# One decoder layer in split fp32r on one core: the seven-product form for the two halves of token chunk 0 in the gate and up projections

## The chip, the cores and the metric

The kernel runs on one core of a Trainium2 chip. The metric is device time in microseconds of one launch, the median of the runs, lower is better. Engines are named as in the profile: PE is TensorE's matmul, PEld its weight load, DVE is VectorE, ACT is ScalarE, POOL is GpSimd, and SP is SyncE, which issues nearly all DMAs here. A DVE instruction, for instance, is one row in DVE's own queue, and each engine runs its queue in order.

## The reference, cut to what matters

A decoder layer for 1024 prompt tokens and 8 x 4 sample tokens, width 1024. The change is in its two SwiGLU blocks; between them stand a gated-delta group, sliding-window attention and a projection, which stay as they are.

```python
def swiglu(h, w_gate, w_up, w_down):
    return (jax.nn.silu(h @ w_gate) * (h @ w_up)) @ w_down

h = rmsnorm(x, lw['norm_ffn1_pre'])
x = x + 0.5 * rmsnorm(swiglu(h, lw['ffn1_w_gate'], lw['ffn1_w_up'], lw['ffn1_w_down']), lw['norm_ffn1_post'])
...                                        # the mixing part
h = rmsnorm(x, lw['norm_ffn2_pre'])
x = x + 0.5 * rmsnorm(swiglu(h, lw['ffn2_w_gate'], lw['ffn2_w_up'], lw['ffn2_w_down']), lw['norm_ffn2_post'])
gate = jax.nn.sigmoid(x @ lw['ple_gate'])  # then the per-layer embedding
```

w_gate and w_up are 1024 x 2816, w_down is 2816 x 1024, all float32.

## The kernel before

**Tiling.** The 1056 tokens lie as columns in three chunks: chunk 0 has 288, chunks 1 and 2 have 384 each. The model width is eight row tiles of 128 (k = 0 to 7). Weights are the stationary operand, 128 x 128 at a time, and tokens the moving one. To keep float32 accuracy every operand is split into a high and a low fp32r half (`hhi`/`hlo` for tokens, the two halves of a `wsp` tile for weights), and a product takes three matmuls: high x high, high x low, low x high (`mm3` at L136 to L138, `mm3p` at L353 to L355). The splitting of weights is one cast on ACT (L128) and one subtraction on DVE (L129) for each 128 x 1024.

**Gate and up (`ffn_up`).** The 2816 output rows are eleven groups of 256, that is two tiles j = 0, 1 of 128. Group 0 is done for all three chunks the plain way (`classic`: 24 matmuls for a chunk, a tile j and a weight). Then chunks 1 and 2 are turned into the operands of a seven-product form (Winograd's variant of Strassen's) of a 2 x 2 block product: the blocks are the two halves of k, the two tiles j, and the two chunks as the two column halves. `half_sums` makes the token sums: in place in chunk 2's upper half of k, and in three tiles `th`. For each later group and each weight, `units` loads 1 MB (`raw`) and makes four `wsp` tiles: the two plain ones and the sums; `seven` does seven products of 12 matmuls of 384 columns, 84 instead of 96, in three accumulators `a`, `b`, `c_` of the `ax` ring, with DVE and ACT adding up between. Chunk 0 goes beside them the plain way: 48 matmuls of 288 columns for each group and weight (`c0a`, `c0b`; banks of the `mm` ring, three of them). In the last group chunk 0 is left out of `seven` and done by `classic` at the end. Results go to `scr_h` in HBM (`out`, L399).

**Order.** The program is written in the order of the work; a scheduler lays the instructions of each engine out by priority and by what it expects to be ready, and each engine then runs its row strictly in order. The first feed-forward takes the chunks in the order 0, 1, 2, the second in 1, 2, 0. Loads and writes stand in one row on SP.

**Down (`ffn_down`).** For each chunk 22 tiles `gt` are read back from `scr_h` (the first ones in one piece, `ga`, the others through a ring `gr` of four) and split on ACT (L548) and DVE (L549); w_down is loaded and split on the way.

**Memory.** Pools lie on a stack. `fq`, `fp` and `th` belong to gate and up; `yd` and `gp` (with all 22 `gt`) take their place afterwards, so the first write to a tile there waits for the last user of what lay there before. A small pool `tp`, open all the time, holds norm temporaries.

Of the kernel before, what the change touches and what calls it, by code (L numbers as in the profile page):

```python
# [8 lines left out]
F32 = mybir.dt.float32  # L9
# [8 lines left out]
P = 128  # L18
GPB = 22
# [15 lines left out]
def emit(tc, A):  # L35
# [11 lines left out]
    tp = pool(name="tp", bufs=2)  # L47
# [167 lines left out]
    def apply_norm(c, x1, r, gain, H, hp=None):  # L215
# [3 lines left out]
        for d in range(KT):  # L219
            if hp and d % 2:  # L220
                hf = hp.tile([P, 384], F32, name=nm("hf"), tag="hfx", bufs=2)[:, :n]
# [4 lines left out]
            tt(lo[:, d, :], hf, hi[:, d, :].bitcast(F32), ALU.subtract)  # L226
# [132 lines left out]
    def half_sums(H, T, fp):  # L359

        (h1, l1), (h2, l2) = H[1], H[2]
        sgt = lambda: fp.tile([P, 384], F32, name=nm("hs"), tag="sg", bufs=SGB)
        for k in range(4):
            b12, b11, b22, b21 = [sgt() for _ in range(4)]
            for t, hh, ll, q in ((b12, h2, l2, k), (b11, h1, l1, k), (b22, h2, l2, k + 4), (b21, h1, l1, k + 4)):
                tt(t, f32(hh[:, q, :]), f32(ll[:, q, :]), ALU.add)
            t3, t2 = sgt(), sgt()
            tt(t3, b22, b12, ALU.subtract)
            tt(b12, b12, b11, ALU.subtract)
            tt(t2, b22, b12, ALU.subtract)  # L370
            tt(b21, b21, t2, ALU.subtract)
            S.copy(h2[:, k, :], b12)  # L372
            tt(l2[:, k, :], b12, f32(h2[:, k, :]), ALU.subtract)
            for i, t in enumerate((t2, t3, b21)):
                S.copy(T[i][:, 0, k, :], t)
                V.tensor_tensor(T[i][:, 1, k, :], t, f32(T[i][:, 0, k, :]), ALU.subtract)
            yield
# [3 lines left out]
    def ffn_up(H, wg, wu, fq, fp, scr, order, opent, hooks={}):  # L381
# [47 lines left out]
        T = opent()  # L429
        for _ in half_sums(H, T, fp):  # L430
            pass
        h0, h1, h2 = H[0], H[1], H[2]
        B = lambda h, o: (lambda k: (h[0][:, o + k, :], h[1][:, o + k, :]))
        TT = lambda i: (lambda k: (T[i][:, 0, k, :], T[i][:, 1, k, :]))
        b11, b21, t1, b22, c0a, c0b = B(h1, 0), B(h1, 4), B(h2, 0), B(h2, 4), B(h0, 0), B(h0, 4)
        n0 = CH[0][1]
# [17 lines left out]
        def seven(us, f, with0):  # L454
# [6 lines left out]
            a, b, c_ = [axbank()[:, :384] for _ in range(3)]  # L461
# [10 lines left out]
            u2 = f.tmp()  # L472
            tt(u2, s1, b, ALU.add)
            pr(c_, q12, 0, t1, True, True)
            pr(b, q34, 0, TT(1), False, True, True)
            u3 = f.tmp()
            tt(u3, s1, b, ALU.add)  # L477
            tt(u3, u3, c_, ALU.add)
            f.sum(1, 2, u3)
            pr(a, u0, 4, b21, False, True, True)  # L480
            f.direct(0, 1, a)
            pr(b, u1, 4, TT(2), False, True, True)
            tt(s1, s1, b, ALU.add)
            f.sum(1, 1, s1)
            pr(c_, q34, 4, b22, False, True, True)
            tt(u2, u2, c_, ALU.add)
            f.sum(0, 2, u2)

        for g in range(1, NG):
# [3 lines left out]
            class Gate:  # L493
                def tmp(self):
                    return sgt(1)

                def c0(self, j, ps):
                    sg[0, j] = sgt(0)
                    S.activation(sg[0, j], ps, AF.Silu)

                def direct(self, j, c, ps):
                    sg[c, j] = sgt(c)
                    S.activation(sg[c, j], ps, AF.Silu)

                def sum(self, j, c, t):
                    sg[c, j] = t
                    S.activation(t, t, AF.Silu)

            class Up:
                def tmp(self):  # L510
                    return fq.tile([P, 384], F32, name=nm("ut"), tag="ut", bufs=4)

                def c0(self, j, ps):
                    self.direct(j, 0, ps)

                def direct(self, j, c, ps):
                    tt(sg[c, j], sg[c, j], ps, ALU.mult)
                    out(sg[c, j], c, 2 * g + j)

                sum = direct  # L520

            for w, f in ((wg, Gate()), (wu, Up())):
                seven(units(raw(w, g)), f, g < NG - 1)
# [4 lines left out]
    def ffn_down(wd, gp, scr, order, yt, finish, after, wide, rate):  # L528
# [3 lines left out]
        def load_g(c):  # L532
# [8 lines left out]
            for f in range(NF):  # L541
                gt = gp.tile([P, 2, 384], F32R, name=nm("gt"), tag="gt")[:, :, :n]
# [105 lines left out]
    ycur[0] = ycur[1] = ypc.__enter__()  # L648
# [1184 lines left out]
```

## Time and profile before

| | us |
|---|---|
| median of 3 runs | 2372.03 (2371.21 to 2372.98) |
| the profiled execution | 2367.41 |
| its span | 2365.7 |
| PE busy | 2252.4 |
| gate and up of the first feed-forward, to its last matmul | to about 506 |
| gate and up of the second, to its last matmul | about 1450 to 1941 |

In the table times within the execution count from the start of the span. Matmuls are pipelined, so that the duration of one (0.33 us at 384 columns) is longer than the step from one start to the next; the step is what counts in a series. A row in which several instructions of one kind were merged (x6) runs from the start of the first to the end of the last. What stands in brackets at the end of a row is the idle time of the engine before it and what ended it. The profile's PEclk is the share of full clock that was granted to TensorE.

### The profile page before, as it was taken

Reading aid. Unit: us, or ns where it says so; the run is one execution under the profiler, and the core shown is the slowest. Engines: PE = TensorE matmul, PEld = TensorE weight load, DVE = VectorE, ACT = ScalarE, POOL = GpSimd, SP = SyncE. Lnnn points to the kernel's source line nnn. Section 1 sums busy time; section 2 is a strip of 40 time slices with the busy share of each in tenths; the row PEclk is TensorE's granted clock in tenths of the full one; section 3 lists DMA queues with packets and bytes.
Section 4 is the critical chain, followed back from the end, with each engine's and each line's share of the span. In section 5 each row is a group of like instructions: output and inputs, shape, how many; then the busy total and the mean of one; then the engine's idle time right before and its main releaser. Section 6 shows DMA issues by size and latency. Waiting matters only on the chain.

```text
span 2365.7 us, 36438 instructions
## 1 busy us (share of the span) xinstructions
PE 2252.4 (95%) x14212; PEld 2142.4 (91%) x14212; DVE 1421.6 (60%) x2992; ACT 920.9 (39%) x1862; POOL 78.4 (3%) x150
## 2 busy tenths in 40 slices
PE   7999999989999699979999998999999999999998
PEld 6999999989999698878888798999999999999876
DVE  6755555555775549992456578965555464746536
ACT  6323222245453335532335555332322233534421
POOL 0000000000000004220010000000000000000000
PEclk9999999999999799978999998999999999999999
DMA  6122222276554426645654366122222256545401
GB/s 238 65 100 79 72 79 78 86 224 211 196 176 157 125 70 199 199 132 162 181 168 126 100 215 219 58 77 86 73 69 76 77 191 202 186 153 168 148 19 56
DMA packets 312658, 313.16 MB, mean 132 GB/s; under 512 B 25929, under 2 KB 295313, under 8 KB 312470
## 3 DMA queue, kind: packets, MB, share of 16 engines
q1 hardware_dynamic: 312486, 310.84, 40.5%
q8 instruction: 112, 1.84, 0.3%
q14 instruction: 60, 0.49, 0.1%
HBM read 235.57 MB, written 77.81 MB: 132 GB/s over the span
## 4 chain that ended last, share of the span: by engine, by line
PE 77%; DVE 13%; DMA 5%; ACT 3%; issue 2%; SPq 0%; DVEq 0%; ACTq 0%; POOL 0%; POOLq 0%
PE ax L353 8%; PE ax L354 8%; PE ax L355 8%; PE mm L353 8%; PE mm L355 8%; PE mm L354 8%; PE mm L136 5%; PE mm L137 5%; PE mm L138 5%; DMA gr<-scr_h 3%; PE mm L1735 1%; PE mm L1731 1%; PE mm L1732 1%; DVE cy L1026 1%; PE ax L986 1%
## 5 line engine op out<-in xcount | busy, mean ns | idle before, releaser
L129 DVE TENSOR_TENSOR wsp<-raw,wsp 128x1024 fp32r<-128x1024 f32 (+1 forms) x290 | 342.1, 1181 | 282.1 <-ACT wsp L128 281.0
L128 ACT CAST wsp<-raw 128x1024 fp32r<-128x1024 f32 (+1 forms) x290 | 292.9, 1014 | 325.5 <-PE mm L355 184.8
L353 PE MATMUL mm<-gt,wsp 128*128 128x384 f32 (+1 forms) x1056 | 341.8, 324 | 14.6 <-ACT gt L548 7.3
L355 PE MATMUL mm<-gt,wsp 128*128 128x384 f32 (+1 forms) x1056 | 340.8, 323 | 1.7 <-DVE wsp L129 1.6
L354 PE MATMUL mm<-gt,wsp 128*128 128x384 f32 (+1 forms) x1056 | 341.5, 323 | 0.0
L136 PE MATMUL mm<-hhi,wsp 128*128 128x384 f32 (+1 forms) x784 | 264.8, 338 | 10.2 <-ACT po L779 8.7
L138 PE MATMUL mm<-hhi,wsp 128*128 128x384 f32 (+1 forms) x784 | 261.7, 334 | 13.3 <-DVE wsp L129 9.9
L137 PE MATMUL mm<-hlo,wsp 128*128 128x384 f32 (+1 forms) x784 | 264.3, 337 | 0.0
L353 PE MATMUL ax<-hhi,wsp 128*128 128x384 f32 x640 | 214.6, 336 | 3.8 <-ACT hhi L372 3.8
L354 PE MATMUL ax<-hlo,wsp 128*128 128x384 f32 x640 | 214.5, 335 | 0.1
L353 PEld LDWEIGHTS mm<-gt,wsp 128*128 128x128 f32 x1056 | 199.9, 189 | 15.6 <-ACT gt L548 12.7
L355 PE MATMUL ax<-hhi,wsp 128*128 128x384 f32 x640 | 213.9, 335 | 0.0
L355 PEld LDWEIGHTS mm<-gt,wsp 128*128 128x128 f32 x1056 | 199.8, 189 | 2.7 <-DVE wsp L129 2.3
L354 PEld LDWEIGHTS mm<-gt,wsp 128*128 128x128 f32 x1056 | 200.0, 189 | 0.8 <-DVE gt L549 0.3
L128 ACT CAST wsp<-st 128x1024 fp32r<-128x1024 f32 x80 | 84.2, 1053 | 268.5 <-PE ax L355 264.8
L354 PE MATMUL mm<-hlo,wsp 128*128 128x288 f32 x576 | 169.8, 295 | 0.0
L353 PE MATMUL mm<-hhi,wsp 128*128 128x288 f32 x576 | 169.8, 295 | 0.0
L355 PE MATMUL mm<-hhi,wsp 128*128 128x288 f32 x576 | 169.7, 295 | 0.0
L138 PEld LDWEIGHTS mm<-hhi,wsp 128*128 128x128 f32 x784 | 153.4, 196 | 15.9 <-DVE wsp L129 10.1
L136 PEld LDWEIGHTS mm<-hhi,wsp 128*128 128x128 f32 x784 | 153.7, 196 | 13.5 <-ACT po L779 9.5
L353 PE MATMUL ax<-th,wsp 128*128 128x384 f32 x480 | 161.1, 336 | 0.6 <-DVE sg L477 0.6
L354 PE MATMUL ax<-th,wsp 128*128 128x384 f32 x480 | 160.4, 334 | 0.0
(457 smaller groups left out, 4460.2 us busy)
## 6 DMA issues: line engine op xcount, KB each, us to landing
raw<-in_ffn_w_down_dram SPq DMA_DIRECT2D x48, 1024.0 KB
raw<-in_ffn_w_gate_dram SPq DMA_DIRECT2D x24, 1024.0 KB
raw<-in_ffn_w_up_dram SPq DMA_DIRECT2D x24, 1024.0 KB
raw<-in_ffn_w_down_dram SPq DMA_DIRECT2D x24, 768.0 KB
scr_h<-sg SPq DMA_DIRECT2D x88, 192.0 KB
gr<-scr_h SPq DMA_DIRECT2D x80, 192.0 KB
raw<-in_w_out_dram SPq DMA_DIRECT2D x12, 1024.0 KB
xr<-scr_x SPq DMA_DIRECT2D x12, 768.0 KB
```

The lines of the kernel that those rows point to most:

```text
L128: S.copy(hi, src)
L129: V.tensor_tensor(lo, src, hi.bitcast(F32), ALU.subtract)
L136: TE.matmul(ps, lhsT=wh, rhs=xh, start=(i == 0), stop=False)
L137: TE.matmul(ps, lhsT=wh, rhs=xl, start=False, stop=False)
L138: TE.matmul(ps, lhsT=wl, rhs=xh, start=False, stop=(i == n - 1))
L353: TE.matmul(ps, lhsT=wh, rhs=xh, start=(first and i == 0), stop=False, skip_group_check=on)
L354: TE.matmul(ps, lhsT=wh, rhs=xl, start=False, stop=False, skip_group_check=on)
L355: TE.matmul(ps, lhsT=wl, rhs=xh, start=False, stop=(last and i == n - 1), skip_group_check=on)
L986: TE.matmul(po[:, (kv * 2 + i) * 64:(kv * 2 + i + 1) * 64], lhsT=pSs[kv][:, i, b, :], rhs=vb[b][:, kv * 64:kv * 64 + 64], start=(b == kb0) ...
L1026: stt(y[:, :L], xb[:, j:j + L], scT[:, t, 24 + j:25 + j], y[:, :L], ALU.mult, ALU.add)
L1731: TE.matmul(pg[:m], lhsT=xh, rhs=u[:, 0, ks], start=(k == 0), stop=False)
L1732: TE.matmul(pg[:m], lhsT=xh, rhs=u[:, 1, ks], start=False, stop=False)
```

## The change

Chunk 0 gets the seven-product form too, with its two halves of 144 columns as the two column halves. `half_sums` makes its sums as well (in place in the second half's upper k, and in three small tiles), after those of chunks 1 and 2. `seven` runs over a list of operand sets, first the one of 384 columns, then the one of 144, product by product; the narrow set has its accumulators in the `mm` ring. This holds for groups 1 to 9; group 10 runs the wide set alone, and `whole_rows` gives chunk 0 its plain rows back for the `classic` at the end. Since the sums need memory, `tp` is closed during gate and up (after group 0) and opened again behind it, `bias_rows` moves behind the first down phase, the `gt` tiles lie in two pools of eleven (`gq` lowest, `gp` on top of `yd`), and the pools of the last part are laid out anew.

```diff
-GPB = 22
+GPB = 11
...
-    tp = pool(name="tp", bufs=2)
+    class Cur:
+        def open(self, name): ...
+        def close(self): ...
+    tp = Cur()
...
-    def half_sums(H, T, fp):
+    def half_sums(H, T, T0, fp):
+        for Ts, c1, o1, c2, o2, n in ((T, 1, 0, 2, 0, 384), (T0, 0, 0, 0, 144, 144)):
+            (h1, l1), (h2, l2) = H[c1], H[c2]
+            s1, s2 = slice(o1, o1 + n), slice(o2, o2 + n)
+            for k in range(4):
+                b12, b11, b22, b21 = [sgt() for _ in range(4)]
+                for t, hh, ll, q, sl in ((b12, h2, l2, k, s2), (b11, h1, l1, k, s1), (b22, h2, l2, k + 4, s2),
+                                         (b21, h1, l1, k + 4, s1)):
+                    tt(t, f32(hh[:, q, sl]), f32(ll[:, q, sl]), ALU.add)
...
+    def whole_rows(H, fp):
+        h, l = H[0]
+        a, b = slice(0, 144), slice(144, 288)
         for k in range(4):
...
+            tt(t, t, u, ALU.add)
+            S.copy(h[:, k, b], t)
+            tt(l[:, k, b], t, f32(h[:, k, b]), ALU.subtract)
...
+        SETS = [(384, axbank, operands(1, 0, 2, 0, 384, T)), (144, mmbank, operands(0, 0, 0, 144, 144, T0))]
...
-            pr(a, u0, 0, b11, True, True)
-            s1 = f.tmp()
-            S.copy(s1, a)
-            if with0:
-                for j, u in enumerate((u0, u1)):
-                    p0 = mmbank()[:, :n0]
-                    pr(p0, u, 0, c0a, True, False)
-                    pr(p0, u, 4, c0b, False, True)
-                    f.c0(j, p0)
-            pr(b, q12, 4, TT(0), True, True)
...
+            for (o, (a, b, c_), b11, b21, t1, b22, t2, t3, t4) in st:
+                pr(a, u0, 0, b11, True, True)
+                S.copy(o.s1, a)
+            for (o, (a, b, c_), b11, b21, t1, b22, t2, t3, t4) in st:
+                pr(b, q12, 4, t2, True, True)
+                tt(o.u2, o.s1, b, ALU.add)
+            for (o, (a, b, c_), b11, b21, t1, b22, t2, t3, t4) in st:
+                pr(c_, q12, 0, t1, True, True)
...
-            for w, f in ((wg, Gate()), (wu, Up())):
-                seven(units(raw(w, g)), f, g < NG - 1)
+            for w, f in ((wg, Gate), (wu, Up)):
+                seven(units(raw(w, g)), f, (0, 1) if g < NG - 1 else (0,))
+            if g == NG - 2:
+                whole_rows(H, fp)
...
-                gt = gp.tile([P, 2, 384], F32R, name=nm("gt"), tag="gt")[:, :, :n]
+                gt = (gp if f < GPB else gq).tile([P, 2, 384], F32R, name=nm("gt"), tag="gt")[:, :, :n]
...
-        (1, 0): lambda: dma(cm, A["c_main"][:, 256:]), (2, 0): bias_rows})
+        (1, 0): lambda: dma(cm, A["c_main"][:, 256:])})
...
-    with tc.tile_pool(name="yd", bufs=1) as yd, tc.tile_pool(name="gp", bufs=GPB) as gp:
+    with tc.tile_pool(name="gq", bufs=F // 128 - GPB) as gq, tc.tile_pool(name="yd", bufs=1) as yd, tc.tile_pool(name="gp", bufs=GPB) as gp:
```

How the instructions stand now, at three places. Names carry their tile's number; lines are those of each kernel, 14 to 50 further down after the change (`mm3p` is L353 to L355 before and L367 to L369 after).

First TensorE in group 2, gate, between the first product and what follows it (`hhi_392` is chunk 1, `hhi_208` chunk 0). Before, the last product row of the wide set and the first rows of chunk 0:

```order
L353 MATMUL ax_1294<-hhi_392,wsp_1276 128x384
L354 MATMUL ax_1294<-hlo_393,wsp_1276 128x384
L355 MATMUL ax_1294<-hhi_392,wsp_1276 128x384
L353 MATMUL mm_1311<-hhi_208,wsp_1276 128x288
L354 MATMUL mm_1311<-hlo_209,wsp_1276 128x288
```

And now:

```order
L367 MATMUL ax_1469<-hhi_392,wsp_1447 128x384
L368 MATMUL ax_1469<-hlo_393,wsp_1447 128x384
L369 MATMUL ax_1469<-hhi_392,wsp_1447 128x384
L367 MATMUL mm_1474<-hhi_208,wsp_1447 128x144
L368 MATMUL mm_1474<-hlo_209,wsp_1447 128x144
```

Behind the twelve wide ones stood 48 of 288 columns, and then the other six products of 12; now each run of 12 wide ones is followed by a run of 12 narrow ones, seven times. TensorE's row has 14015 entries for 12719.

Second DVE at the end of the half sums of the first feed-forward. Before, the last sums of chunks 1 and 2 (`hs`, `th`) and what came behind them: the products of chunk 0 (`sg_971`), the first sum of the wide set (L473) and two weight splits (L129):

```order
L371 TENSOR_TENSOR hs_889<-hs_889,hs_895 128x384
L373 TENSOR_TENSOR hlo_561<-hs_886,hhi_560 128x384
L376 TENSOR_TENSOR th_817<-hs_895,th_817 128x384
L376 TENSOR_TENSOR th_819<-hs_889,th_819 128x384
L517 TENSOR_TENSOR sg_971<-sg_971,mm_1121 128x288
L473 TENSOR_TENSOR sg_1012<-sg_944,ax_930 128x384
L129 TENSOR_TENSOR wsp_1088<-st_1092,wsp_1088 128x1024
```

Now the first eight of the 48 operations for chunk 0 (with the last of the wide ones, `th_820`, between them):

```order
L384 TENSOR_TENSOR hs_912<-hhi_208,hlo_209 128x144
L394 TENSOR_TENSOR th_820<-hs_893,th_820 128x384
L384 TENSOR_TENSOR hs_913<-hhi_208,hlo_209 128x144
L384 TENSOR_TENSOR hs_914<-hhi_208,hlo_209 128x144
L384 TENSOR_TENSOR hs_915<-hhi_208,hlo_209 128x144
L386 TENSOR_TENSOR hs_920<-hs_914,hs_912 128x144
L387 TENSOR_TENSOR hs_912<-hs_912,hs_913 128x144
L388 TENSOR_TENSOR hs_921<-hs_914,hs_912 128x144
L394 TENSOR_TENSOR th_822<-hs_920,th_822 128x144
```

And their end, with the first sum of the wide set (L500) and the next weight split behind it:

```order
L391 TENSOR_TENSOR hlo_209<-hs_978,hhi_208 128x144
L394 TENSOR_TENSOR th_821<-hs_987,th_821 128x144
L500 TENSOR_TENSOR sg_1023<-sg_1022,ax_1026 128x384
L394 TENSOR_TENSOR th_823<-hs_981,th_823 128x144
L500 TENSOR_TENSOR sg_1028<-sg_1029,mm_1031 128x144
L143 TENSOR_TENSOR wsp_1225<-st_1229,wsp_1225 128x1024
```

The 48 narrow operations stand between the wide sums and the first sum of products. On TensorE the wide products 1 to 3 of gate, the narrow product 1 and two products of up stand ahead of the narrow products that read `th_821` and `hlo_209`.

Third ACT where gate and up end and the first down phase begins: before, the last two activations (`sg`), the casts of w_down (`wsp`), and then the first casts of `gt`:

```order
L420 ACTIVATE sg_4409<-mm_4359 128x288
L128 CAST wsp_4574<-raw_4572 128x1024
L128 CAST wsp_4601<-raw_4572 128x1024
L420 ACTIVATE sg_4463<-mm_4413 128x288
L128 CAST wsp_4630<-raw_4628 128x1024
L548 CAST gt_4478<-ga_4476 128x288
```

Now the last of eleven casts of `gt`, with the activation of the second tile and the casts of w_down behind them:

```order
L589 CAST gt_5438<-ga_5409 128x288
L589 CAST gt_5441<-gr_5442 128x288
L449 ACTIVATE sg_5390<-mm_5340 128x288
L142 CAST wsp_5507<-raw_5505 128x1024
L142 CAST wsp_5534<-raw_5505 128x1024
L142 CAST wsp_5563<-raw_5561 128x1024
L589 CAST gt_5446<-gr_5447 128x288
```

The first eleven `gt` moved ahead of the second activation and of the weight casts. On SP the first load of w_down (`raw_5505`) moved behind the write of the first of the two products of this end (`sg_5336`); before, `raw_4572` stood ahead of it.

More of the change, by code (lines that the diff above doesn't have):

```diff
@@ L472, in seven @@
[L472 to L485, printed above, removed]
@@ L486, in seven @@
-            tt(u2, u2, c_, ALU.add)
-            f.sum(0, 2, u2)
+            st = []
+            for i in sets:
+                n, bank, (b11, b21, t1, b22, t2, t3, t4) = SETS[i]
+                st.append((f(i), [bank()[:, :n] for _ in range(3)], b11, b21, t1, b22, t2, t3, t4))
+            for (o, (a, b, c_), b11, b21, t1, b22, t2, t3, t4) in st:
[4 more added lines that the diff above has]
+                tt(o.u2, o.s1, b, ALU.add)
@@ L489, in ffn_up @@
+            for (o, (a, b, c_), b11, b21, t1, b22, t2, t3, t4) in st:
+                pr(b, u1, 4, t4, False, True, True)
+                tt(o.s1, o.s1, b, ALU.add)
+                o.done(1, 0, o.s1)
+            for (o, (a, b, c_), b11, b21, t1, b22, t2, t3, t4) in st:
+                pr(c_, q34, 4, b22, False, True, True)
+                tt(o.u2, o.u2, c_, ALU.add)
+                o.done(0, 1, o.u2)
         for g in range(1, NG):
@@ L526, in ffn_up, with ffn_down @@
             classic(0, NG - 1, j, ug, uu)
-    def ffn_down(wd, gp, scr, order, yt, finish, after, wide, rate):
+    def ffn_down(wd, gp, gq, scr, order, yt, finish, after, wide, rate):
         NF = F // 128
@@ L1630, in emit @@
     cvz.__exit__(None, None, None)
+    tp.close()
     H3 = {}
```

143 lines of the change are left out of this document (85 added, 58 removed).

## The prediction

> **What bounds the kernel.** First the page: the span and the engines' shares.
>
> ```profile
> span 2365.7 us, 36438 instructions
> PE 2252.4 (95%) x14212; PEld 2142.4 (91%) x14212; DVE 1421.6 (60%) x2992; ACT 920.9 (39%) x1862; POOL 78.4 (3%) x150
> ```
>
> TensorE is busy nearly everywhere, and every matmul (PE) has a weight load of its own (PEld): 14212 of each. The second view, busy time by stretch, says how tightly. The columns are the stretch, its length, then the busy time and the count of instructions of each engine, and the granted clock.
>
> ```profile
> core 0: us, PE busy (x) PEld busy (x) DVE busy (x) ACT busy (x) POOL busy (x), PEclk, DMA share, GB/s
> 83.00:136.80 53.80, 52.20 (x328) 50.52 (x327) 44.93 (x79) 20.63 (x34) 0.00 (x0) 1.00 0.25 87
> 136.80:157.75 20.95, 20.95 (x134) 20.95 (x133) 10.18 (x14) 6.84 (x10) 0.00 (x0) 1.00 0.07 24
> ...
> 1517.80:1566.40 48.60, 46.39 (x278) 45.35 (x277) 43.50 (x77) 20.47 (x33) 0.00 (x0) 0.96 0.19 65
> ```
>
> The row of 136.80 to 157.75 is one *stage*: one weight (gate or up) of one group, without an idle moment on PE, while DVE works half the time and ACT a third. (The two long rows are the first groups of the two feed-forwards.) So a stage costs what its matmuls cost, and the third view, single matmuls in order of time, gives their price: from one start to the next, since durations overlap.
>
> ```profile
> 290.65 0.33 PE L353 MATMUL ax<-hhi,wsp 128*128 128x384 f32 x1
> ...
> 292.73 0.33 PE L353 MATMUL ax<-th,wsp 128*128 128x384 f32 x1
> ...
> 299.76 0.29 PE L353 MATMUL mm<-hhi,wsp 128*128 128x288 f32 x1
> ...
> 303.36 0.29 PE L353 MATMUL mm<-hhi,wsp 128*128 128x288 f32 x1
> ```
>
> Twelve matmuls of 384 columns lie between the first two rows: 2.08/12 = 0.1733 us each. Twenty-seven of 288 lie between the last two: 3.60/27 = 0.1333 us. A stage has 84 and 48 of them: 14.56 + 6.40 = 20.96 us, the 20.95 of the windows. Their difference is 0.0417 us for 100 columns, so 0.0133 us of each is not columns.
>
> **The stages.** In nine groups of each feed-forward, for both weights (36 stages), chunk 0's 48 matmuls of 288 columns become 84 of 144. Columns fall from 13824 to 12096 a stage; matmuls, and with them weight loads, rise by 36. The whole question is what a matmul of 144 columns costs. No row of before has that width between new weights. Bounded from below by the line through the two widths it is 0.0733 us; then 84 cost 6.16 us, 0.24 less than now. The nearest rows from the other side are matmuls in series, each with 128 new weight columns and few columns of its own:
>
> ```profile
> 590.51 0.83 PE L591 MATMUL fx<-cx,ss 128*128 128x1 f32 x6 [0.51 <-DVE ss L209]
> ...
> 1256.34 1.17 PE L986 MATMUL ax<-vtok,pS 128*128 128x64 f32 x9
> ...
> L986 PE MATMUL ax<-vtok,pS 128*128 128x64 f32 x240 | 29.7, 276 | 2.1 <-ACT pS L980 2.1
> ```
>
> A merged row runs from the first start to the last end, so with the last one's own 0.28 us (the group row's mean; 0.26 at one column) taken off: (0.83 - 0.26)/5 = 0.115 us with 1 column, (1.17 - 0.28)/8 = 0.111 with 64. The price does not depend on the columns: it is that of the weight load. These are plain fp32; the chunk's operands are fp32r, and for that type the trace has 128 columns beside 512:
>
> ```profile
> 2300.47 0.39 PE L1732 MATMUL mm<-wsp,hhi 128*128 128x512 f32 x1
> 2300.70 0.22 PE L1734 MATMUL ax<-identr,hhi 128*128 128x128 f32 x1
> 2300.76 0.45 PE L1735 MATMUL mm<-wsp,hlo 128*128 128x512 f32 x1
> 2301.05 0.22 PE L1737 MATMUL ax<-identr,hlo 128*128 128x128 f32 x1
> 2301.11 0.44 PE L1731 MATMUL mm<-wsp,hhi 128*128 128x512 f32 x1
> 2301.39 0.39 PE L1732 MATMUL mm<-wsp,hhi 128*128 128x512 f32 x1
> ```
>
> 512 columns behind settled weights take 0.23 us (first to second row). A narrow one and the wide one behind it take 0.35 (second to fourth) and 0.34 (fourth to sixth), so the narrow one costs 0.11 to 0.12, although its successor is *recorded* 0.06 later: the successor then waits for its weights, which shows as 0.45 or 0.44 instead of 0.39. I take **0.113 us** for 144 columns, and keep 0.073 and 0.120 as ends. Then 84 x 0.113 = 9.49 us against 6.40: **+3.09 us a stage, +111 us in 36 stages** (ends -9 and +132). The neighbours of 384 columns don't help: they hide only their successor's load.
>
> The Trainium skill, page "TensorE: Matmul & The Clock Gate", section "LDWEIGHTS (loading the stationary operand)", gives a load time of the number of weight columns over 1.2, in ns, whatever the rows: 107 ns for 128 columns. The rows above agree with it to a few ns, and by it alone the sum would be 84 x 0.107 = 8.99, so +2.59 a stage and +93 us, an estimate.
>
> What rides along in a stage is nine more DVE operations of 144 columns with up, five with gate, and a few on ACT. They lie beside PE, which has 24 us a stage now against 10.2 of DVE; without that cover they would cost 2 us a stage. A bank that is read on DVE and accumulated into again has two runs of twelve matmuls and more between, 3 us at least.
>
> **The first groups.** Chunk 0's half sums, 48 DVE operations of 144 columns, stand on DVE behind the 48 of chunks 1 and 2, and products 2 and 3 of the narrow set wait for them. Before, the same place held 96 matmuls of chunk 0 in gate and up that needed no sums: 12.8 us of filler for PE, now gone.
>
> ```profile
> 78.58 1.96 DVE L366 TENSOR_TENSOR hs<-hhi,hlo 128x384 f32<-128x384 f32 x4
> ...
> 83.02 0.33 PE L353 MATMUL ax<-hhi,wsp 128*128 128x384 f32 x1
> ...
> 103.45 1.23 DVE L129 TENSOR_TENSOR wsp<-raw,wsp 128x1024 fp32r<-128x1024 f32 x1
> 104.59 0.55 DVE L371 TENSOR_TENSOR hs<-hs,hs 128x384 f32<-128x384 f32 x1
> ...
> 105.53 1.02 DVE L376 TENSOR_TENSOR th<-hs,th 128x384 fp32r<-128x384 f32 x2
> ...
> 1503.35 1.19 DVE L226 TENSOR_TENSOR hlo<-hf,hhi 128x288 fp32r<-128x288 f32 x3
> ...
> 1517.84 0.34 PE L353 MATMUL ax<-hhi,wsp 128*128 128x384 f32 x1
> ...
> 1541.31 1.22 DVE L129 TENSOR_TENSOR wsp<-raw,wsp 128x1024 fp32r<-128x1024 f32 x1
> ```
>
> DVE steps are 0.47 us at 384 columns ((1.96 - 0.55)/3) and 0.37 at 288 ((1.19 - 0.45)/2), so 0.22 at 144: 10.6 us for 48, up to 14 if each waits for the one before (0.29). I take 11. PE starts the group at 83.02; what it can do before those sums is 62 matmuls of 384 and 36 of 144, 10.7 + 4.1 = 14.8 us: to 97.8. DVE ended the wide sums at 106.5; the weight split of 1.14 us at 103.45 now stands behind them: 105.3, and with 11 more 116.3. PE waits 18.5 us, of which it idled 1.6 before (53.80 - 52.20): +17. In the second feed-forward the start is 1517.84 (to 1532.6) and the wide sums end 0.47 after 1541.31, with 11 more 1552.8: 20.2, less 2.2 idle before: +18. **+35 us** together (ends 0, were the sums hidden, and 41). Halved clock after these waits: +3, by the rows that follow.
>
> **Into the down phases.** The same view of stretches as above, and rows of SP and ACT in order of time:
>
> ```profile
> 506.30:513.80 7.50, 0.29 (x3) 0.05 (x1) 1.68 (x2) 1.49 (x3) 0.00 (x0) 0.65 1.02 337
> 513.80:518.80 5.00, 4.96 (x21) 4.96 (x22) 4.98 (x14) 4.42 (x13) 0.00 (x0) 0.51 0.85 258
> 1941.50:1946.70 5.20, 0.19 (x2) 0.00 (x1) 1.70 (x3) 1.61 (x3) 0.00 (x0) 0.89 1.06 365
> 1946.70:1952.30 5.60, 5.60 (x17) 5.30 (x18) 5.60 (x12) 4.74 (x11) 0.00 (x0) 0.50 0.89 266
> ```
>
> ```profile
> 505.19 1.13 SPq L565 DMA_DIRECT2D raw<-in_ffn_w_down_dram  x2
> ...
> 510.80 1.04 ACT L128 CAST wsp<-raw 128x1024 fp32r<-128x1024 f32 x1 [6.41 <-DMA raw<-in_ffn_w_down_dram]
> ...
> 513.35 0.76 ACT L548 CAST gt<-ga 128x288 fp32r<-128x288 f32 x2 [1.51 <-DMA scr_h<-sg]
> ```
>
> PE stands still for 7.2 and 5.0 us, then runs at half clock for 5.0 and 5.6, which costs 2.5 and 2.8 more. The first gt tile lay in memory that the last write of sg to scr_h still read. Now it doesn't, and the first eleven casts are done inside the last 12.8 us of gate and up. What is late next is the first weight tile: its load now stands on SP behind the write of the first product of those 12.8 us, some 5 us ahead of their end, and takes 5.6 (505.19 to 510.80), with the cast of 1.04 behind it. A gap of about 2 us is left, too short for the halved clock if the gap of 1.6 us in the first group is a guide. That gives -5 and -2.5 at the first place, -3 and -2 at the second: **-12** (ends 0 and -17). The bias rows behind the down phase and the new layout at the end I cost at nothing; PE's work there covers them, and a wait for one small load would be 4 us at worst.
>
> **Sum.** 111 + 35 + 3 - 12 = +137 us. The profiled execution took 2367.4 us; the median of the runs, 2372.0, is 4.6 above it. So 2367.4 + 137 + 4.6 = **2509 us**.
>
> **Rivals.** (a) The sums of chunk 0 are hidden: 2509 - 38 = 2471. For it speaks that chunk 0 is ready first in the first feed-forward; against it, that its sums stand on DVE behind the wide ones. Chance 0.13. (b) The load and the fixed 0.013 us add up, 0.120: 2509 + 21 = 2530, chance 0.14. (c) Columns and the fixed 0.013 alone count, 0.073: 2509 - 111 - 9 = 2389; the series above speak against it, 0.05. (d) Faster: the narrow matmul costs its recorded step, 0.06 us at 128 columns and so 0.065 at 144, the load being wholly hidden. 84 x 0.065 = 5.46, -0.94 a stage, -34: 2509 - 111 - 34 = 2364. It decides from 0.067 us down, where 36 stages pay for the +26 of the rest. The 0.34 and 0.35 us of the pairs speak against it: 0.04. The Trainium skill, same page, section "Back-to-back issue gap", has N/2.4 + 2.5 ns for isolated matmuls, 62.5 at 144, close to (d), and about 81 ns a matmul of 128 columns with loads; the trace's 0.11 to 0.12 at 128 columns agrees with neither. That the matmuls aren't added is excluded by the program's order.
>
> **Numbers.** My forecast has 0.62, between 2490 and 2522. 2466 to 2544 takes in (a), (b) and the ends of the stalls. A difference of 0.2% is about what a measurement of this kernel can tell from none. Faster: (d), 0.04. Within 0.2%: 0.02, a price between (c) and (d). Slower: the rest, 0.94.
>
> **What would show it.** Stages of 24.0 us with PE without idle, and 1.36 us for twelve matmuls of 144 columns, show the main term; 20.7 would show (c). A wait of PE on th or hlo near 98 to 116 us, with DVE busy throughout, shows the second, none shows (a). A gap under 3 us before the first gt matmul shows the third. I am wrong above all if the 144-column step is not set by the load, which would show as a step below 0.10 us.

## The result and the profile after

| | before | changed |
|---|---|---|
| median, us | 2371.62 (4 runs, 2369.55 to 2372.98) | 2493.07 (4 runs, 2489.87 to 2495.11) |
| ratio, with 95% interval | 1 | 1.0527 (1.0494 to 1.056) |
| the profiled execution, us | 2367.41 | 2495.11 |
| its span, us | 2365.7 | 2493.4 |

The changed kernel is 121 us slower by the medians and 127.7 us by the two profiled executions. (That of before lay 4.2 us below its median of these runs, that of the changed kernel 2.0 above its own.) The page:

```profile
span 2493.4 us, 39497 instructions
PE 2372.8 (95%) x15508; PEld 2255.7 (90%) x15508; DVE 1516.8 (61%) x3336; ACT 951.4 (38%) x1974; POOL 79.9 (3%) x150
```

TensorE has 1296 more matmuls (36 stages of 36 more) and 120 us more busy time; its share is 95% as before. To see where the time went I took the start of a few matmuls that both programs have, and subtracted:

| from the start of ... to the start of ... | before, us | changed, us | difference |
|---|---|---|---|
| the program, to the first wide matmul of group 1 | 83.02 | 83.27 | +0.25 |
| that one, to the last wide matmul of group 10 (first feed-forward) | 410.45 | 483.26 | +72.82 |
| that one, to the first matmul on gt | 20.37 | 14.74 | -5.63 |
| that one, to the last matmul on gt | 265.13 | 265.09 | -0.03 |
| that one, to the first matmul of the mixing projection | 567.73 | 556.07 | -11.67 |
| that one, to the first wide matmul of group 1 (second feed-forward) | 171.15 | 171.84 | +0.69 |
| that one, to the last wide matmul of group 10 | 410.73 | 486.04 | +75.32 |
| that one, to the first matmul on gt | 18.13 | 15.09 | -3.04 |
| that one, to the last matmul of the program (second down phase and last part) | 409.79 | 408.76 | -1.03 |

Now the views that the prediction had read, of the changed kernel. First busy time by stretch: the two first groups, and between them one stage of group 2.

```profile
83.27:152.58 69.31, 56.59 (x337) 52.75 (x337) 55.69 (x133) 24.60 (x51) 0.00 (x0) 0.85 0.12 36
169.75:193.80 24.05, 24.05 (x170) 24.05 (x170) 12.49 (x21) 6.62 (x11) 0.00 (x0) 1.00 0.18 54
1574.27:1646.40 72.13, 58.68 (x339) 54.08 (x337) 57.60 (x135) 25.46 (x52) 0.00 (x0) 0.83 0.11 34
```

A stage takes 24.05 us with PE never idle. It was 20.95. The first groups (two stages each) take 69.31 and 72.13 us, at a mean clock of 0.85 and 0.83. Next, single matmuls in order of time, at the seam of two runs of twelve:

```profile
169.75 0.38 PE L367 MATMUL ax<-th,wsp 128*128 128x384 f32 x1
...
171.56 0.34 PE L368 MATMUL ax<-th,wsp 128*128 128x384 f32 x1
171.74 0.34 PE L369 MATMUL ax<-th,wsp 128*128 128x384 f32 x1
171.92 0.23 PE L367 MATMUL mm<-th,wsp 128*128 128x144 f32 x1
171.98 0.27 PE L368 MATMUL mm<-th,wsp 128*128 128x144 f32 x1
172.09 0.28 PE L369 MATMUL mm<-th,wsp 128*128 128x144 f32 x1
...
173.10 0.28 PE L369 MATMUL mm<-th,wsp 128*128 128x144 f32 x1
173.21 0.38 PE L367 MATMUL ax<-hhi,wsp 128*128 128x384 f32 x1
173.43 0.34 PE L368 MATMUL ax<-hlo,wsp 128*128 128x384 f32 x1
```

Within the run a narrow matmul takes 0.112 us (ten steps from 171.98 to 173.10). The first of a run is followed after 0.06 only, since its own weights were loaded beside the wide matmul in front. At the other end the bill comes: the first wide matmul behind the run needs 0.22 us to the next start, where the others need 0.175. This pair of runs takes 173.21 - 169.75 = 3.46 us; seven such pairs make the stage.

Third, what PE waited for in the first group of the first feed-forward, from 83 to 125 us (engine, name and line; what it waited for; us in all, times, longest):

```profile
PE ax L367 <- ACT hhi L390: 7.2, 3, 3.8
PE mm L367 <- ACT hhi L390: 3.2, 3, 1.1
PE mm L367 <- ACT th L393: 1.6, 1, 1.6
PE ax L368 <- DVE hlo L391: 0.6, 2, 0.4
```

All of it is half sums. L390 is the cast of a sum that is written in place. And the waits where the down phase begins (579 to 600 us) and behind its end (851 to 893), of the changed kernel:

```profile
PE mm L367 <- ACT wsp L142: 1.7, 1, 1.7
PE mm L369 <- DVE wsp L143: 0.5, 1, 0.5
...
PE ax L114 <- DMA oh<-in_c_swa_dram: 3.0, 1, 3.0
PE mm L150 <- ACT wsp L142: 2.7, 2, 2.3
PE ax L796 <- DMA st<-in_conv_w_dram: 2.4, 1, 2.4
```

The same view of before, behind the end of its first down phase (786 to 816 us), which the prediction had not read:

```profile
PE mm L138 <- DVE wsp L129: 9.9, 1, 9.9
PE mm L136 <- ACT po L779: 8.7, 1, 8.7
```

These two long waits, 18.6 us together, are gone in the changed kernel, and the smaller ones above have come in. The -11.67 us of the table is what is left of that gain.

### The profile page after: what moved, and what is told of

The parts are those of the page before. It is cut to its first block, busy times and chain, and to the rows that moved or that the text cites. A ratio compares the mean times of both kernels' runs of the same rounds, so it can differ in the third digit from the quotient of the medians.

```text
span 2493.4 us, 39497 instructions
## 1 busy us (share of the span) xinstructions
PE 2372.8 (95%) x15508; PEld 2255.7 (90%) x15508; DVE 1516.8 (61%) x3336; ACT 951.4 (38%) x1974; POOL 79.9 (3%) x150
## 4 chain that ended last, share of the span: by engine, by line
PE 77%; DVE 13%; DMA 4%; ACT 3%; issue 2%; SPq 0%; DVEq 0%; POOL 0%; ACTq 0%; POOLq 0%
PE mm L369 10%; PE mm L368 10%; PE mm L367 9%; PE ax L367 8%; PE ax L368 8%; PE ax L369 8%; PE mm L150 4%; PE mm L151 4%; PE mm L152 4%; PE mm L1781 1%; PE mm L1777 1%; DMA gr<-scr_h 1%; PE mm L1778 1%; DVE cy L1071 1%; PE ax L1031 1%
## 5 line engine op out<-in xcount | busy, mean ns | idle before, releaser
L142 ACT CAST wsp<-raw 128x1024 fp32r<-128x1024 f32 (+1 forms) x290 | 293.1, 1013 | 385.1 <-PE mm L369 328.8
L367 PE MATMUL mm<-gt,wsp 128*128 128x384 f32 (+1 forms) x1056 | 342.9, 325 | 6.1 <-ACT wsp L142 3.7
L369 PE MATMUL mm<-gt,wsp 128*128 128x384 f32 (+1 forms) x1056 | 342.2, 325 | 2.5 <-DVE wsp L143 2.4
L367 PE MATMUL ax<-hhi,wsp 128*128 128x384 f32 x640 | 223.3, 349 | 14.6 <-ACT hhi L390 14.1
L369 PE MATMUL ax<-hhi,wsp 128*128 128x384 f32 x640 | 215.6, 337 | 0.0
L367 PEld LDWEIGHTS mm<-gt,wsp 128*128 128x128 f32 x1056 | 199.2, 189 | 7.0 <-ACT wsp L142 4.2
L369 PEld LDWEIGHTS mm<-gt,wsp 128*128 128x128 f32 x1056 | 199.4, 189 | 4.0 <-DVE wsp L143 3.6
L143 DVE TENSOR_TENSOR wsp<-st,wsp 128x1024 fp32r<-128x1024 f32 x80 | 98.0, 1225 | 167.8 <-ACT wsp L142 167.8
L142 ACT CAST wsp<-st 128x1024 fp32r<-128x1024 f32 x80 | 83.9, 1049 | 272.2 <-PE mm L369 219.5
L367 PE MATMUL ax<-th,wsp 128*128 128x384 f32 x480 | 168.0, 350 | 0.0
L368 PE MATMUL ax<-th,wsp 128*128 128x384 f32 x480 | 163.2, 340 | 0.7 <-DVE th L394 0.4
L369 PE MATMUL ax<-th,wsp 128*128 128x384 f32 x480 | 162.8, 339 | 0.0
L150 PEld LDWEIGHTS mm<-hhi,wsp 128*128 128x128 f32 x784 | 151.6, 193 | 11.5 <-ACT wsp L142 3.1
L368 PE MATMUL mm<-hlo,wsp 128*128 128x144 f32 x576 | 159.9, 278 | 0.0
L369 PE MATMUL mm<-hhi,wsp 128*128 128x144 f32 x576 | 159.4, 277 | 0.0
```

The lines of the kernel that those rows point to most:

```text
L142: S.copy(hi, src)
L143: V.tensor_tensor(lo, src, hi.bitcast(F32), ALU.subtract)
L150: TE.matmul(ps, lhsT=wh, rhs=xh, start=(i == 0), stop=False)
L367: TE.matmul(ps, lhsT=wh, rhs=xh, start=(first and i == 0), stop=False, skip_group_check=on)
L368: TE.matmul(ps, lhsT=wh, rhs=xl, start=False, stop=False, skip_group_check=on)
L369: TE.matmul(ps, lhsT=wl, rhs=xh, start=False, stop=(last and i == n - 1), skip_group_check=on)
```

## The experiments

Three questions were open. What sets the price of a narrow matmul: its load, or its columns? Is the loss in the first groups PE waiting for chunk 0's sums? And which part of the memory's rearrangement brought the gains, two of them expected and one not? Each ratio below is against runs of before that went with its own set; their medians were 2367.71 us (the first groups, the first kernel with chunk 0 plain, the two pools alone and the late bias rows), 2369.86 (the three on the price) and 2369.67 (the other three). Medians of different sets can thus be compared to about 4 us.

### The price of the narrow matmul

**192 columns.** Nearly every matmul of the narrow set reads 48 columns more; the sums take the first 144 as before.

```diff
-        SETS = [(384, axbank, operands(1, 0, 2, 0, 384, T)), (144, mmbank, operands(0, 0, 0, 144, 144, T0))]
...
+            cut = lambda x, s: x[:, s:min(s + 192, 8 * 288)]
+            return lambda k: (cut(hf, (r + k) * 288 + o), cut(lf, (r + k) * 288 + o))
...
+        SETS = [(384, axbank, operands(1, 0, 2, 0, 384, T)), (144, mmbank, wide0)]
```

> The changed kernel with 192 instead of 144 moving columns in nearly all matmuls of the narrow set; the added 48 columns are not used. Theory (the weight load sets the step of a narrow matmul): no change, 24.05 us a stage and 2493 us. Rival (columns set it, at 0.000417 us each): 84 x 0.020 = +1.7 us a stage, 25.7 us, and 2493 + 60 = 2553 us.

Measured: 2495.58 us, ratio 1.0532 (1.0478 to 1.0585).

**96 columns.** The first matmul into each bank keeps 144, all others take 96, so this kernel leaves out most terms of the last 48 columns of each half.

```diff
+        cut = 96 if ps.shape[-1] == 144 else None
...
+            ps, xh, xl = (ps[:, :cut], xh[:, :cut], xl[:, :cut]) if cut else (ps, xh, xl)
```

> The changed kernel with 96 instead of 144 moving columns in all matmuls of the narrow set but the first into each bank, so that most terms of the last 48 columns of each half of chunk 0 are left out. Theory (load): no change, 24.05 us a stage, 2493 us. Rival (columns): 81 x 0.020 = -1.6 us a stage, 22.4 us, and 2493 - 58 = 2435 us.

Measured: 2500.02 us, ratio 1.055 (1.0496 to 1.0605).

One stage of group 2 in the view of stretches, first with 192 and then with 96 columns:

```profile
179.48:203.46 23.98, 23.98 (x170) 23.98 (x170) 13.99 (x25) 5.37 (x8) 0.00 (x0) 1.00 0.20 58
```

```profile
176.35:200.40 24.05, 24.05 (x170) 24.05 (x170) 13.99 (x25) 5.36 (x8) 0.00 (x0) 1.00 0.19 59
```

23.98 us with 192 columns, 24.05 with 144, 24.05 with 96. Twice the columns cost nothing. So columns don't set the price of a narrow matmul; they would have made 3.3 us a stage between the two kernels. A fixed price of any matmul, whatever weights it loads, is a rival that these two runs leave. A row of before, with weight tiles of 64 x 64 and 64 columns, at a granted clock of 1.00, speaks against it:

```profile
1135.27 0.67 PE L1465 MATMUL ax<-lS,xs 64*64 64x64 f32 x8
```

With the last one's own 0.22 us taken off, that is (0.67 - 0.22)/7 = 0.064 us a matmul, where the prediction's row with 64 columns and weight tiles of 128 x 128 gave 0.111. The price goes with the size of the weight tile: it is that of the load.

**Alternating.** Wide and narrow matmuls with the same weights follow each other one by one.

```diff
+    def mm3x(runs, u, first, last, on=False):
+        n = 4
+        for i in range(n):
+            for w, x in ((0, 0), (0, 1), (1, 0)):
+                for ps, xs in runs:
+                    TE.matmul(ps, lhsT=kslc(u[0], u[1] + i)[w], rhs=xs(i)[x], ...)
...
+            mm3x([(s[1][0], s[2]) for s in st], (u0, 0), True, True)
             for (o, (a, b, c_), b11, b21, t1, b22, t2, t3, t4) in st:
-                pr(a, u0, 0, b11, True, True)
```

> The changed kernel with the wide and the narrow set alternating matmul by matmul with the same weights, instead of runs of twelve. Theory: a load can be one matmul ahead and no more, so a narrow matmul between wide ones still costs 0.113 to 0.118 us, as the 128-column ones between 512-column ones do: 84 x (0.173 + 0.115) = 24.2 us a stage, 2493 to 2505 us. Rival (the wide neighbours hide the narrow one's load): 84 x (0.173 + 0.065) = 20.0 us a stage, 2493 - 146 = 2347 us.

Measured: 2494.77 us, ratio 1.0528 (1.0471 to 1.0585), and a stage of 24.06 us. The matmuls of that kernel in order of time:

```profile
181.86 0.38 PE L376 MATMUL ax<-th,wsp 128*128 128x384 f32 x1
182.08 0.23 PE L376 MATMUL mm<-th,wsp 128*128 128x144 f32 x1
182.15 0.38 PE L376 MATMUL ax<-th,wsp 128*128 128x384 f32 x1
182.37 0.23 PE L376 MATMUL mm<-th,wsp 128*128 128x144 f32 x1
182.44 0.38 PE L376 MATMUL ax<-th,wsp 128*128 128x384 f32 x1
```

Every narrow matmul now shows the step of 0.07 us that the prediction's rival (d) hoped for, and every wide one behind it shows 0.22. A pair takes 0.29 us, as 0.175 and 0.11 did apart. A recorded step of a narrow matmul between wide ones is no price; only the pair is. Were the load hidden beside any wide neighbour, a pair would take 0.247 us (0.1733 and the 0.0733 of the line through the two widths, an estimate). That the weights of the two are the same doesn't help either: each matmul still has its load.

### The first groups

Group 1 does chunk 0 the plain way again, and chunk 0's sums are made behind it; the narrow set runs in groups 2 to 9.

```diff
-        half_sums(H, T, T0, fp)
+        half_sums(H, [(T, 1, 0, 2, 0, 384)], fp)
...
-                seven(units(raw(w, g)), f, (0, 1) if g < NG - 1 else (0,))
+                seven(units(raw(w, g)), f, (0, 1) if 1 < g < NG - 1 else (0,), g == 1)
+            if g == 1:
+                half_sums(H, [(T0, 0, 0, 0, 144, 144)], fp)
```

> The changed kernel, but group 1 does chunk 0 the plain way and its half sums are made behind group 1: the narrow set runs in groups 2 to 9. Theory: the first groups' loss beyond the stage price (69.3 and 72.1 us for two stages, where two later ones take 48.1 and before took 45.3 and 46.5) is PE waiting for the 48 sums of chunk 0. With 96 matmuls of filler it goes: -37 us, and 4 stages fewer at 3.10 give -12.4: 2493 - 49 = 2444 us. Rival: the wait moves to the start of group 2, where the same 48 operations stand: 2493 - 12 = 2481 us.

Measured: 2450.64 us, ratio 1.0353 (1.0337 to 1.037). The first groups in the view of stretches:

```profile
84.48:128.93 44.45, 42.85 (x266) 42.01 (x265) 43.49 (x103) 21.50 (x43) 0.00 (x0) 1.00 0.14 44
1549.74:1596.54 46.80, 44.48 (x267) 43.48 (x265) 45.27 (x108) 22.65 (x44) 0.00 (x0) 0.96 0.13 41
```

44.45 and 46.80 us, where before took 45.3 and 46.5, and the first stage of group 2 takes 23.99: no wait moved there. Gate and up are 47.9 and 50.0 us above before, which is 16 stages of 3.1. So the loss was PE waiting beside DVE's sums, and 96 matmuls that need no sums fill it. Between the profiles gate and up got 50.3 us shorter than in the changed kernel, as forecast; the median is 6.6 us above the forecast, by parts outside gate and up that weren't traced.

### The memory

**Chunk 0 plain, the rest as changed.** In groups 1 to 9 `seven` runs the wide set alone and does chunk 0's 48 matmuls of 288 columns behind its first product, as before.

```diff
-                seven(units(raw(w, g)), f, (0, 1) if g < NG - 1 else (0,))
-            if g == NG - 2:
-                whole_rows(H, fp)
+                seven(units(raw(w, g)), f, (0,), g < NG - 1)
```

> The changed kernel's memory and pools, with chunk 0 computed the plain way in groups 1 to 9 as before (its narrow tiles are allocated and unused). Theory: everything lost is the seven-product form of chunk 0 (gate and up: +72.8 and +75.3 us between the profiles), and everything won is the memory: -8.7 us where the two down phases begin and -11.7 us between the first down phase and the mixing projection. Then gate and up take 410.5 us again each, and the time is 2371.6 - 20.4 = 2351 us. Rival: the -11.7 us are a chance of when loads land after the longer gate and up; then 2363 us. Second rival: closing the small pool during gate and up costs something of its own there; then above 2363.

Measured: 2381.97 us, ratio 1.0059 (1.0043 to 1.0075): 0.6% slower than before. By the landmarks of the table above it had won 5.5 and 1.8 us at the down phases and 16.9 in the mixing part, and had lost 35 us between the mixing projection and the end of the second gate and up (616.9 for 581.9). What PE waited for at the start of that stretch (1454 to 1492 us):

```profile
PE mm L150 <- ACT wsp L142: 8.3, 1, 8.3
PE fx L186 <- DVE ss L223: 8.0, 1, 8.0
PE ax L367 <- ACT wsp L142: 5.8, 1, 5.8
PE fx L199 <- DVE dg L194: 2.7, 1, 2.7
```

The first wide product of group 1 stood in PE's row ahead of chunk 0's norm, which in turn was late on DVE. In the changed kernel's row it doesn't. What this kernel lacked of the changed one in memory was one tile, vt, that only the narrow set uses.

**The same with vt.** The tile is allocated and never written.

```diff
+        fq.tile([P, 3, 144], F32, name=nm("vt"), tag="vt", bufs=1)
         for g in range(1, NG):
```

> The first of these kernels (chunk 0 plain in groups 1 to 9) with one tile more, never written: the small tile vt of 128 x 3 x 144 in the lowest pool of gate and up, that the changed kernel has there. Theory: without it the pool above lay 1.7 KB lower than in the changed kernel, over memory that the mixing part uses longer, so the second weight tiles of the second feed-forward's group 0 came late and group 1's products were put in front of the norm of chunk 0; that cost the 35 us between the mixing projection and the end of the second gate and up (616.9 against 581.9 us). With it the stretch takes 582 us again, and the memory alone gives 2369 - 20 = 2348 us. Rival (the wait has to do with leaving out the narrow set itself): 2382 us again.

Measured: 2354.49 us, ratio 0.9939 (0.9925 to 0.9954). The stretch takes 582.6 us; the loss of 35 us is gone. That the tile decides is shown. Which memory the pool above it then met was inferred from the rows and not tried apart. Against the forecast of 2348 the kernel is 6 us slow; the second down phase took 270.3 us in its profile, 5.2 more than before. There TensorE ran at half clock from 2033.8 to 2040.6 us, around a wait of 2.8 us on DVE, and from 2146.4 to 2149.9; before had full clock in this phase but for its first 5.6 us. What made that wait wasn't traced.

**Only the two pools for gt**, on the kernel before.

```diff
-GPB = 22
+GPB = 11
...
-                gt = gp.tile([P, 2, 384], ...
+                gt = (gp if f < GPB else gq).tile([P, 2, 384], ...
...
-    with tc.tile_pool(name="yd", bufs=1) as yd, tc.tile_pool(name="gp", bufs=GPB) as gp:
+    with tc.tile_pool(name="gq", bufs=F // 128 - GPB) as gq, tc.tile_pool(name="yd", bufs=1) as yd, tc.tile_pool(name="gp", bufs=GPB) as gp:
```

> The kernel before with one edit: the 22 gt tiles in two pools of eleven, one under yd and one on top; the bias rows, the small pool and chunk 0 stay as before. Theory: both gains come from this split, since SP's row now has the small loads of the mixing part and the third weight tile of w_in ahead of the write of the last chunk; 2351 to 2355 us, and no wait of 10 us of PE behind the first down phase. Rival: only the start of the down phases is helped by the split (2363 us), the mixing part by the late bias rows.

Measured: 2379.66 us, ratio 1.0049 (1.0034 to 1.0064). Theory and rival were both wrong in part. The mixing part won 20.6 us, more than in the changed kernel, so that gain does come from the split. But the down phases began 7.0 and 7.4 us later than before, and behind the last gt matmul 19.3 us were lost. The waits of PE at these two places (506 to 522, and 2210 to 2234 us):

```profile
PE mm L353 <- DMA gr<-scr_h: 14.2, 1, 14.2
...
PE mm L1731 <- ACT wsp L128: 11.2, 1, 11.2
PE ax L1711 <- DMA pin<-in_p_prompt_dram: 2.7, 1, 2.7
```

At the first place SP issues the load of the first gt tiles (`ga`) at 514.4 us, behind the last write of sg to scr_h at 508.6; in the changed kernel it stands ahead of the last three of these writes.

**The same with the new layout of the last part.**

```diff
-    with tc.tile_pool(name="pe", bufs=1) as pe, tc.tile_pool(name="pp", bufs=1) as pp, tc.tile_pool(name="pr", bufs=1) as pr:
-        ple(pp, pr, pe)
+    with tc.tile_pool(name="pp", bufs=1) as pp, tc.tile_pool(name="pe", bufs=1) as pe, tc.tile_pool(name="pr", bufs=1) as pr, \
+            tc.tile_pool(name="pt", bufs=1) as pt_:
+        ple(pp, pe, pr, pt_)
```

> The kernel before with the gt tiles in two pools and with the pools of the last part laid out as in the changed kernel; the rest is as before. Theory: the 19.3 us that the split alone lost behind the last gt matmul are a wait for memory, and the new layout of the last part takes them back, while the down phases still start 7 us late each: 2369 + 12 - 19 = 2362 us, 145 us behind the last gt matmul. Rival (the loss there has another cause): 2380 us.

Measured: 2357.53 us, ratio 0.9952 (0.9938 to 0.9966). The last part takes 144.2 us again (before 144.7, with the split alone 164.0), and the down phases still begin 8.0 and 8.7 us late. (The profiled execution took 2366.68 us, 9 above the median, and the parts are read from it.) So the split needs the new layout at the end, and something else in the changed kernel lets gt start early. It isn't vt: the first kernel of this section had no vt, and its down phases began 5.5 and 1.8 us earlier than before. What it had besides the split and the layout is the small pool that is closed and reopened, chunk 0's tiles for the sums, and the late bias rows; these weren't taken apart.

**Only the late bias rows**, on the kernel before.

```diff
-        (1, 0): lambda: dma(cm, A["c_main"][:, 256:]), (2, 0): bias_rows})
+        (1, 0): lambda: dma(cm, A["c_main"][:, 256:])})
...
+    bias_rows()
     MGT, MLE = cm[:, 0:128], cm[:, 128:256]
```

> The kernel before with one edit: the bias rows are made behind the first down phase and not in group 2. Theory: nothing is won, because the write of the last chunk still stands ahead of the next weight tile on SP: 2371.6 us within 3. Rival (the late bias rows bring the -11.7 us): 2360 us.

Measured: 2367.81 us, ratio 1.0002 (0.9986 to 1.0017). Nothing, as expected. The two long waits behind the first down phase, 9.9 and 8.7 us, are as before in its trace, and PE waits for none of the bias rows' loads there. A likely reason, then, is that PE stood still at this place in any case.

**The bias rows early**, on the kernel with chunk 0 plain and vt.

```diff
-        (1, 0): lambda: dma(cm, A["c_main"][:, 256:])})
+        (0, 7): bias_rows, (1, 0): lambda: dma(cm, A["c_main"][:, 256:])})
...
-    bias_rows()
```

> The kernel with chunk 0 plain and the tile vt, but the bias rows made in group 0 of the first feed-forward, while the small pool is still open. Theory: behind the first down phase the bias rows cost TensorE a wait of 3.4 us and most of the 10 us of half clock behind it, so their move saves 4 to 8 us: 2340 to 2344 us. Rival (another wait takes its place there, or one in group 0): 2348 us or more.

Measured: 2339.53 us, ratio 0.9877 (0.986 to 0.9894): the fastest of all, 30 us below before and 154 below the changed kernel. The waits of PE behind the first down phase, first with the late rows (805 to 818 us) and then with the early ones (783 to 830):

```profile
PE ax L114 <- DMA oh<-in_c_swa_dram: 3.1, 1, 3.1
PE ax L807 <- DMA st<-in_conv_w_dram: 2.5, 1, 2.5
PE mm L150 <- ACT xb L1068: 0.7, 1, 0.7
```

```profile
PE mm L150 <- ACT wsp L142: 2.3, 1, 2.3
PE mm L150 <- ACT bs L1381: 0.5, 1, 0.5
```

The first wait of the second list, 2.3 us, stands in the kernel with the late rows too, at 785 us. By the landmarks that part of the program is 13.0 us shorter. With the late rows 3.1 and 2.5 us were waited for, and TensorE ran at half clock from 811.8 to 822.0:

```profile
811.80:822.00 10.20, 6.65 (x23) 5.18 (x24) 4.61 (x13) 2.73 (x8) 1.21 (x7) 0.50 0.58 193
```

PE was busy for 6.65 of these 10.2 us, so the halved clock cost about 3.3, an estimate; the three waits of the first list come to 6.3. The expectation had 4 to 8 for the whole and was too low: it had counted one wait of 3.4 us, and the second of the waits went as well. Some 3 us of the 13.0 are not placed.

## Why the prediction was right, and where it was not

The time lies 16 us below the forecast and inside its range, and the two terms that make up most of it came for the reason given. By its steps:

**The stages** were forecast at +3.09 us each, +111 us. Measured: 24.05 - 20.95 = 3.10, and 36 of them are 111.6 us. A narrow matmul was to cost 0.113 us; it costs 0.112. The step that carried it, the price taken from series whose load is everything, holds: the runs with 96, 144 and 192 columns have one price. The rivals (c) and (d), by columns and by the recorded step, fall with the runs of 96 and 192 columns and with the alternating one; (b), 0.120 us, falls with the step of 0.112. The Trainium skill, page "TensorE: Matmul & The Clock Gate", section "LDWEIGHTS (loading the stationary operand)", gives the number of weight columns over 1.2, in ns, so 107 ns for 128 columns, an estimate; these runs agree within 5 ns. The section "Back-to-back issue gap" has about 81 ns for a matmul of 128 columns with a load each; no series of matmuls here is so fast, and the measurement decides.

**The first groups** were forecast at +35 us of waiting and +3 of halved clock. Measured against the stage price: 69.31 - 48.10 = 21.2 us, of which before had 45.3 - 41.9 = 3.4, so +17.8; in the second feed-forward 24.0 less 4.6, so +19.4. Together +37.2 for a forecast of 38, and rival (a) falls. What sets the end was forecast rightly: DVE, whose row of sums PE stands behind. In the first row below DVE works nearly without a pause, and PE's last wait for a sum ends at 116.1 us, where the forecast had 116.3. The second row is the stretch of halved clock.

```profile
83.50:116.90 33.40, 20.68 (x92) 16.84 (x91) 33.12 (x92) 13.77 (x34) 0.00 (x0) 0.75 0.02 6
100.13:120.61 20.48, 12.29 (x39) 10.40 (x40) 18.59 (x63) 8.44 (x23) 0.00 (x0) 0.50 0.00 1
```

How PE spends the time up to there was forecast wrongly. It was to do 98 matmuls without a stop and then stand still for 18.5 us. Instead it was idle for 69.31 - 56.59 = 12.7 us in all (13.5 in the second feed-forward, for 20.2), nearly all in eight pieces from 89 us on, and ran at half clock from 100.1. Of the 12.6 us in the waits shown 7.8 are the wide set's, on its in-place sums: the prediction let PE pass through these products without a wait, although the filler that had covered those sums was gone. This cost little, because PE had to wait for DVE at 116 us in any case. Only what is left behind that wait counts: 90 matmuls were done by then and not 98, which is 1.0 us, and 4.5 us of halved clock remain, which cost about 2.3 (both by the matmuls' prices, an estimate). That such errors, and an excess before of 3.4 us where the prediction took off 1.6, cancel to within 1 us is luck. The cause, chunk 0's matmuls no longer filling the time of the sums, is shown by the run that puts them back.

**Into the down phases** the forecast was -12 us: the gaps -5 and -3, the clock behind them -2.5 and -2. The gaps gave -5.6 and -3.0, with the weight tile as what is late next, as said (1.7 us on L142). The clock's share didn't come: from the first to the last gt matmul it was 265.13 us before and 265.09 after at the first place, and 265.10 and 264.69 at the second. At the first place the halved clock is gone all the same. The ten us from the first gt matmul on, before and in the changed kernel:

```profile
513.84:523.84 10.00, 10.00 (x59) 10.00 (x60) 6.91 (x16) 6.56 (x16) 0.00 (x0) 0.76 0.88 284
```

```profile
581.27:591.27 10.00, 9.53 (x69) 9.30 (x70) 6.82 (x9) 6.06 (x11) 0.00 (x0) 1.00 0.96 296
```

At full clock instead of 0.76, PE starts 69 matmuls for 59. That is a lead of 1.4 us, and by the thousandth of the 1584 matmuls of this phase it is gone; to what was not traced. At the second place the clock halved again in the changed kernel, behind a gap of 2.0 us, which the prediction had called too short for it:

```profile
2076.45:2079.86 3.41, 3.21 (x10) 3.21 (x11) 1.28 (x2) 0.00 (x0) 0.00 (x0) 0.50 1.03 354
```

**At nothing** stood the bias rows and the new layout. That step failed. The mixing part got 11.7 us shorter. The split of gt alone gives 20.6 us there, on the kernel before, and the late bias rows, once the long waits that covered them are gone, take part of it back. That the small loads and the staging tile po of that part now lie in memory that the down phase gives up early is read from the rows and not shown apart. Before, the first copy into po stood on ACT behind the whole norm of the last chunk, and PE waited 9.9 and 8.7 us. The rows of ACT in order of time, before:

```profile
813.15 1.04 ACT L634 CAST hhi<-hf 128x384 fp32r<-128x384 f32 x2 [1.43 <-DVE hf L633]
814.10 0.24 ACT L1314 CAST uba<-raw 128x64 fp32r<-128x64 f32 x1
814.24 0.69 ACT L779 COPY po<-mm 128x288 f32<-128x288 f32 x2
```

and in the changed kernel, where it stands ahead of that norm:

```profile
850.93 0.40 ACT L824 COPY po<-mm 128x288 f32<-128x288 f32 x1 [3.14 <-PE mm L152]
...
855.21 0.40 ACT L824 COPY po<-mm 128x288 f32<-128x288 f32 x1 [1.51 <-PE mm L152]
855.51 0.53 ACT L219 ACTIVATE ss<-yd 128x384 f32<-128x384 f32 x1
```

The bias rows were costed at nothing, at worst a wait of 4 us. In the plain kernel with vt their place costs 15 us by the medians, 13.0 of it in the mixing part.

**The sum** was 137 us over the profiled execution and measured 127.7. The difference is the -11.7 us that no term held, less 3 us that the down phases won short of their forecast. The forecast also put the median 4.6 us above the profile, and here it lay 2.0 below.

## What to carry to other kernels

Count matmuls before columns. With a new weight tile each, 96, 144 and 192 columns cost one price here, that of the load, and 288 cost more; the two meet at some 240 columns, an estimate (0.0133 us and 0.000417 a column reach 0.113 there). The scheme saved an eighth of the columns by halving their width, and 36 more loads a stage cost more than that. Plain work beside a scheme that needs prepared operands is filler for the time of the preparation, and taking it away needs another filler. When one engine's row sets the end of a stretch, forecast that row; how the waiting engine spends the time before it matters little. And when memory is rearranged on a stack of pools, compare every engine's row at each seam: a tile of 1.7 KB that nobody writes was worth 35 us in one stretch here, and some 27 us of the median.

## What the runs showed of the hardware

Between two wide matmuls a narrow one shows a step of 0.07 us and its successor one of 0.22 instead of 0.175: the trace puts the price of a load on the matmul behind. Several short waits can halve the clock where one doesn't. In the first group before, one wait of 1.6 us left it at 1.00; in the changed kernel waits of 1.4, 2.0 and 0.4 us and the start of one of 3.8 were followed by 20.5 us at 0.50. Single gaps differ as well: behind 1.7 us before the first gt matmul of the changed kernel the clock stayed at 1.00, behind 2.0 us at the second place it was 0.50 for 3.4 us. No run tried for the threshold.
